# Reordered changes of sub-layer with unread products, half-depth s jobs, pair copies and a shared last norm in a three-part decoder layer

## The chip, the cores and the metric

The kernel runs on one core of one Trainium2 chip. The metric is the time of one execution on the device in microseconds (us). The core has TensorE (PE in the profile, with PEld for the loading of its stationary operand), VectorE (DVE), ScalarE (ACT), GpSimd (POOL) and the queue that issues most transfers (SP). Each engine works through its own instructions in the order written and waits for others at semaphores.

## The reference

One layer with three sub-layers acts on x of 256 tokens by 2048 columns. A conditioning vector c gives a shift, a scale and a gate for each sub-layer through a matrix `w_cond` of 2048 x 18432.

```python
mod = (silu(c) @ w_cond + b_cond).reshape(B, 3, 3, 2048)
u = modulate(x, mod[:, 0, 0], mod[:, 0, 1])            # u = x * (1 + scale) + shift
h = (silu(u @ w1) * (u @ w3)) @ w2                     # FFN1, inner width 5632
x = layer_norm(ALPHA * x + 0.5 * (1 + mod[:, 0, 2]) * h, ln_g[0], ln_b[0])
u = modulate(x, mod[:, 1, 0], mod[:, 1, 1])
q, k, v, s = split(u @ w_in, 4)                        # four times 1024 columns
h = concat([diff_attention(q, k, v, lam), s5_branch(s)]) @ w_out
x = layer_norm(ALPHA * x + (1 + mod[:, 1, 2]) * h, ln_g[1], ln_b[1])
...                                                    # FFN2, like FFN1, with the third rows
```

Everything is float32. The `s5_branch` is a linear recurrence over the tokens in 64 groups with a gated output.

## The kernel before, in words

**Products.** A float32 weight piece of 128 x 1024 (512 KB) is loaded as `raw`, cast by ScalarE to a shorter type as `hi` (L691), and VectorE makes the remainder `lo` = raw - hi. The activations u are kept in the same way as `Uh` and `Ul`, transposed (columns on partitions), in 16 tiles k of 128 columns. A piece is then used in three products per tile: hi with Uh, hi with Ul, lo with Uh. A piece with its products is a job; FFN jobs have 12 products of 512 columns, jobs for s, q and k have 24 of 256 columns. All VectorE and TensorE instructions are recorded through a helper and carry its line, L106 in the profile.

**The order of the work** is written out by the class `Stream`. `run` takes the jobs in order; after each it does what is due (`later(n, f)` puts f behind the n-th job from now) and splits pieces ahead (`split_to`; at most AHEAD = 4 pieces stand in the rings `hi` and `lo`). Jobs marked `hold` split nothing behind them. `pay` issues the low parts that are owed. Between jobs, `drain` puts steps of the conditioning vector (`gv`: a 128 x 1024 product and sum on VectorE) where an account of VectorE's and TensorE's time allows it (LIM, GVM); it rests for the last QUIET jobs of a sub-layer.

**Changes of sub-layer.** The last output block runs its 4 jobs for token half t = 0 first, then for t = 1 in two column halves; `residual` adds gate x product to Y and takes the norm's statistics, `ln_token` ends them (L844), then normalises Y: the first half by ScalarE (L865), the second by VectorE. `turn` transposes pairs of k tiles of Y on TensorE (`ps<-ident,Y`), and `turn_mod` makes `uf` (scale and shift, ScalarE L743), `Uh` and `Ul` of them. Pairs 0 and 1 are turned ahead of the first job of the next sub-layer, the others between the jobs that follow.

**s.** `mk_s(t, hf)` computes 128 columns t of s from half hf of the depth; two t share one PSUM bank. After hf = 1 ScalarE copies the tile out as `sT` (L1147) and issues its transfer to DRAM, `sD`; GpSimd's queue loads it back regrouped as `U` for the recurrence after each fourth t.

**FFN, k-outer.** Part of the w1 and w3 products run pass by pass over the depth and are summed in `kosum`. `up_post` multiplies silu with the up part, and two `turned` steps transpose the result into H.

**Ends.** `z(db)` multiplies Y by the gate and adds ALPHA x (Z_AT gives the jobs). The third sub-layer's norm is two VectorE operations per chunk, then the transfer to the output.

## Time and profile before

| | |
|---|---|
| median of 3 runs | 1914.42 us (1912.57 to 1918.12) |
| profiled execution | 1912.22 us |
| its span | 1910.4 us |
| TensorE busy | 1858.5 us, 97% |
| VectorE busy | 1488.1 us, 78% |
| ScalarE busy | 889.4 us, 47% |
| GpSimd busy | 65.0 us, 3% |
| moved by DMA | 532.36 MB, mean 279 GB/s |

Times in rows count from the start of the span. A row of the timeline has start, duration, engine, line, operation, tiles written and read, shape and number, and in brackets the idle time ahead of it and what ended it. FFN1 runs to about 783 us, the mixer to 1147, FFN2 from there. A product's listed duration overlaps the next one's; the distance of two starts is what a product takes.

### The profile page before, as it was taken

What the parts mean: (1) busy time and instruction counts of PE and PEld (TensorE: products, weight loads), DVE (VectorE), ACT (ScalarE), POOL (GpSimd) and SP (SyncE); (2) the same over time, 40 slices, a digit from 0 to 9 for tenths busy, and PEclk for the clock granted to TensorE, in tenths of its full rate; (3) what the DMA queues carried; (4) which work ended last, traced back from release to release, by engine and by line L of the source; (5) the groups of instructions that cost most, each with busy time, mean ns of one, the idle gap of its engine ahead of it and who ended that gap; (6) DMA issues with size and microseconds to landing.
All of it is one profiled execution on the core that took longest, in us unless ns stands there. A gap on an engine that the chain in (4) does not pass through costs nothing.

```text
span 1910.4 us, 25429 instructions
## 1 busy us (share of the span) xinstructions
PE 1858.5 (97%) x9326; PEld 1567.5 (82%) x9326; DVE 1488.1 (78%) x2255; ACT 889.4 (47%) x1211; POOL 65.0 (3%) x119
## 2 busy tenths in 40 slices
PE   6999999999999999899999998999999999999996
PEld 5888878888888888889999886888888888888885
DVE  6889899978888979888998987887876555445468
ACT  3544444465445433634457635544444444344442
POOL 0000000000000000111210000000000000000000
PEclk9999999999999999999999998999999999999998
DMA  9999878889899888798988885998887555565563
GB/s 375 363 338 315 296 247 292 295 306 309 305 347 326 308 323 312 280 337 294 313 268 311 283 309 202 339 357 275 294 279 249 187 188 191 194 215 187 191 233 110
DMA packets 151935, 532.36 MB, mean 279 GB/s; under 512 B 21841, under 2 KB 23297, under 8 KB 150657
## 3 DMA queue, kind: packets, MB, share of 16 engines
q1 hardware_dynamic: 137234, 495.32, 74.3%
q0 software_dynamic: 6512, 23.89, 3.7%
q10 hardware_dynamic: 8064, 11.54, 1.7%
q8 instruction: 73, 1.20, 0.2%
q14 instruction: 52, 0.43, 0.1%
HBM read 513.34 MB, written 17.33 MB: 278 GB/s over the span
## 4 chain that ended last, share of the span: by engine, by line
PE 87%; DVE 6%; DMA 4%; ACT 2%; issue 1%; POOL 0%; SPq 0%; DVEq 0%; ACTq 0%; POOLq 0%
PE ps L106 87%; DVE lo L106 2%; DVE Y L106 2%; DMA raw<-in_f1w_dram 1%; DVE gv L106 1%; ACT hi L691 1%; DMA early<-in_w_cond_dram 1%; DMA raw<-in_wout_dram 0%; DMA U<-sD 0%; DVE st L106 0%; DVE r L106 0%; DMA sD<-sT 0%; DMA early<-in_wc_dram 0%; ACT Y L865 0%; DVE early L106 0%
## 5 line engine op out<-in xcount | busy, mean ns | idle before, releaser
L106 DVE TENSOR_TENSOR lo<-raw,hi 128x1024 fp32r<-128x1024 f32 x630 | 766.3, 1222 | 342.1 <-ACT hi L691 338.5
L691 ACT CAST hi<-raw 128x1024 fp32r<-128x1024 f32 x630 | 661.4, 1053 | 705.8 <-PE ps L106 461.0
L106 PE MATMUL ps<-hi,Uh 128*128 128x512 f32 x1472 | 583.7, 397 | 16.7 <-ACT Uh L318 9.7
L106 PE MATMUL ps<-hi,Ul 128*128 128x512 f32 x1472 | 577.5, 392 | 0.8 <-DVE Ul L106 0.8
L106 PE MATMUL ps<-lo,Uh 128*128 128x512 f32 x1472 | 457.4, 392 | 1.3 <-DVE lo L106 1.3
L106 PEld LDWEIGHTS ps<-hi,Uh 128*128 128x128 f32 x1472 | 278.7, 189 | 77.8 <-ACT Uh L318 10.4
L106 PEld LDWEIGHTS ps<-lo,Uh 128*128 128x128 f32 x1472 | 278.4, 189 | 60.9 <-DVE lo L106 2.0
L106 PEld LDWEIGHTS ps<-hi,Ul 128*128 128x128 f32 x1472 | 279.0, 190 | 58.1 <-DVE Ul L106 1.9
L106 DVE SCALAR_TENSOR_TENSOR gv<-gv,sc 128x1024 f32<-128x1024 f32 x258 | 314.2, 1219 | 1.4 <-DMA gv<-in_w_cond_dram 1.3
L106 PE MATMUL ps<-hi,Hh 128*128 128x512 f32 (+1 forms) x716 | 274.6, 385 | 0.0
L106 PE MATMUL ps<-hi,Hl 128*128 128x512 f32 (+1 forms) x716 | 273.6, 383 | 0.0
L106 PE MATMUL ps<-lo,Hh 128*128 128x512 f32 (+1 forms) x716 | 216.5, 384 | 1.8 <-DVE lo L106 1.8
L106 PEld LDWEIGHTS ps<-lo,Hh 128*128 128x128 f32 x716 | 133.0, 188 | 29.1 <-DVE lo L106 2.6
L106 PEld LDWEIGHTS ps<-hi,Hh 128*128 128x128 f32 x716 | 134.5, 188 | 26.8 <-issue 0.4
L106 PEld LDWEIGHTS ps<-hi,Hl 128*128 128x128 f32 x716 | 134.6, 188 | 26.0
L106 PE MATMUL ps<-Uh,hi 128*128 128x256 f32 x384 | 97.9, 292 | 2.4 <-ACT sT L1147 1.8
L106 PE MATMUL ps<-Ul,hi 128*128 128x256 f32 x384 | 95.7, 286 | 0.1
L106 PEld LDWEIGHTS ps<-Uh,hi 128*128 128x128 f32 x384 | 74.2, 193 | 6.2 <-ACT sT L1147 2.7
L106 PEld LDWEIGHTS ps<-Ul,hi 128*128 128x128 f32 x384 | 74.2, 193 | 0.8 <-DVE Ul L106 0.7
L1010 ACT CAST Hh<-ps 128x512 fp32r<-128x512 f32 x44 | 25.8, 587 | 78.6 <-PE ps L106 78.6
L106 PE MATMUL ps<-Uh,lo 128*128 128x256 f32 x384 | 53.9, 283 | 0.0
L106 DVE TENSOR_TENSOR Hl<-ps,Hh 128x512 fp32r<-128x512 f32 x44 | 30.3, 688 | 30.0 <-ACT Hh L1010 29.7
(229 smaller groups left out, 1393.4 us busy)
## 6 DMA issues: line engine op xcount, KB each, us to landing
raw<-in_f1w_dram SPq DMA_DIRECT2D x264, 512.0 KB, 6.0
raw<-in_f2w_dram SPq DMA_DIRECT2D x264, 512.0 KB, 4.7
gv<-in_w_cond_dram SPq DMA_DIRECT2D x258, 512.0 KB, 7.1
raw<-in_win_a_dram SPq DMA_DIRECT2D x48, 512.0 KB, 6.0
raw<-in_wout_dram SPq DMA_DIRECT2D x32, 512.0 KB, 5.8
early<-in_w_cond_dram SPq DMA_DIRECT2D x28, 512.0 KB, 7.6
s5m<-scrB POOLq DMA_DIRECT2D x8, 1024.0 KB, 8.4
raw<-in_win_v_dram SPq DMA_DIRECT2D x16, 512.0 KB, 4.8
```

The costliest lines, as they stand in the source:

```text
L106: return f(*a, **k)
L691: S.copy(hi, raw)
L1010: S.copy(hh, p)
```

## The change

It has eight parts.

1. `warm(n)` issues n products of 512 columns whose result nothing reads: 16 in the opening, 11 and 3 behind the transposes of t = 0 and t = 1 at the first change, 12 and 3 at the second.
2. At a change only the first quarter of the second token half is normalised at once; `first_turn` turns two pairs, pays, normalises quarter 1, splits the pieces of the next four jobs and normalises quarters 2 and 3 behind their low parts.
3. The last block splits one piece more, ahead of the first residual; the first piece of a sub-layer gets a slab of its own (`hilo`, listed in `firsts`).
4. The first four s jobs run over k tiles 0 to 3 first, all four of them, and then over 4 to 7; the order of the jobs becomes t 0 to 5 first half, t 0 to 3 second half, t 6 and 7 first half, t 4 to 7 second half. Later pairs are turned one job later.
5. s is copied out for two t at once.
6. In the k-outer passes the second `turned` comes two jobs after the first, not one.
7. Y's gate and ALPHA operations come one and two jobs earlier (Z_AT); QUIET is 6 and 5 for 3; GVM of the mixer 0.68 for 0.65.
8. In the last norm, half of the columns of t = 0 and a quarter of t = 1 are done by ScalarE (one operation) and GpSimd (two); VectorE's last 1024 columns of t = 1 are cut as 512, 256, 256.

Line numbers grow: L106 becomes L110, L691 L705, L743 L757, L865 L887.

TensorE at the first change, in its program around the two turnings (`wr` is the tile that the unread products read; `hilo` the slab of the first piece), before:

```order
2719 L106 MATMUL ps<-lo,Hh 128x256 x2
2720 L106 MATMUL ps<-ident,Y 128x128 x8
2721 L106 MATMUL ps<-Uh,hi 128x256
2722 L106 MATMUL ps<-Ul,hi 128x256
2723 L106 MATMUL ps<-Uh,hi 128x256
```

and after:

```order
2720 L110 MATMUL ps<-lo,Hh 128x256 x2
2721 L110 MATMUL ps<-ident,Y 128x128 x4
2722 L218 MATMUL ps<-wr 128x512 x11
2723 L110 MATMUL ps<-ident,Y 128x128 x4
2724 L218 MATMUL ps<-wr 128x512 x3
2725 L110 MATMUL ps<-Uh,hilo 128x256
```

The unread products stand between the transposes of the two token halves and behind the second.

VectorE at the second change, from the end of the norm's statistics of t = 1, before:

```order
1136 L106 SCALAR_TENSOR_TENSOR rs<-q_10788,rs 128x1
1137 L106 TENSOR_SCALAR Y<-Y,mv,rs 128x512 x4
1138 L106 CAST Uh<-uf 128x256
1139 L106 TENSOR_TENSOR Ul<-uf,Uh 128x256 x2
1140 L106 CAST Uh<-uf 128x256
1141 L106 TENSOR_TENSOR Ul<-uf,Uh 128x256 x2
1142 L106 TENSOR_TENSOR lo<-raw,hi 128x1024
1143 L106 CAST Uh<-uf 128x256
1144 L106 TENSOR_TENSOR Ul<-uf,Uh 128x256 x2
1145 L106 TENSOR_TENSOR lo<-raw,hi 128x1024 x4
```

and after:

```order
1143 L110 TENSOR_SCALAR Y<-Y,mv,rs 128x512
1144 L110 CAST Uh<-uf 128x256
1145 L110 TENSOR_TENSOR Ul<-uf,Uh 128x256 x2
1146 L110 CAST Uh<-uf 128x256
1147 L110 TENSOR_TENSOR Ul<-uf,Uh 128x256 x2
1148 L110 TENSOR_TENSOR lo<-raw,hi 128x1024
1149 L110 TENSOR_SCALAR Y<-Y,mv,rs 128x512
1150 L110 TENSOR_TENSOR lo<-raw,hi 128x1024 x2
1151 L110 TENSOR_SCALAR Y<-Y,mv,rs 128x512 x2
1152 L110 TENSOR_TENSOR lo<-raw,hi 128x1024
1153 L110 SCALAR_TENSOR_TENSOR gv,acc<-gv,sc 128x1024
1154 L110 CAST Uh<-uf 128x256
```

Three of the normalisations have moved behind the first casts and between the low parts, and four low parts now stand ahead of the third pair's cast (row 1154), where one stood.

VectorE at the end of the program, behind the second token half's last `rs`, before:

```order
1452 L106 SCALAR_TENSOR_TENSOR rs<-q_16372,rs 128x1
1453 L106 SCALAR_TENSOR_TENSOR Y<-Y,mv,gb 128x512
1454 L106 SCALAR_TENSOR_TENSOR Y<-Y,rs,bb 128x512
1455 L106 SCALAR_TENSOR_TENSOR Y<-Y,mv,gb 128x512
1456 L106 SCALAR_TENSOR_TENSOR Y<-Y,rs,bb 128x512
1457 L106 SCALAR_TENSOR_TENSOR Y<-Y,mv,gb 128x512
1458 L106 SCALAR_TENSOR_TENSOR Y<-Y,rs,bb 128x512
1459 L106 SCALAR_TENSOR_TENSOR Y<-Y,mv,gb 128x512
1460 L106 SCALAR_TENSOR_TENSOR Y<-Y,rs,bb 128x512
```

and after:

```order
1465 L110 SCALAR_TENSOR_TENSOR nm<-mv,rs 128x1
1466 L110 SCALAR_TENSOR_TENSOR Y<-Y,mv,gb 128x512
1467 L110 SCALAR_TENSOR_TENSOR Y<-Y,rs,bb 128x512
1468 L110 SCALAR_TENSOR_TENSOR Y<-Y,mv,gb 128x512
1469 L110 SCALAR_TENSOR_TENSOR Y<-Y,rs,bb 128x512
1470 L110 SCALAR_TENSOR_TENSOR Y<-Y,mv,gb 128x256
1471 L110 SCALAR_TENSOR_TENSOR Y<-Y,rs,bb 128x256
1472 L110 SCALAR_TENSOR_TENSOR Y<-Y,mv,gb 128x256
1473 L110 SCALAR_TENSOR_TENSOR Y<-Y,rs,bb 128x256
```

One chunk of 512 columns has left VectorE, the last is cut in two, and `nm` (ScalarE's bias) is new.

The diff, cut to its core:

```diff
-GVM = (0.57, 0.65, 0.85, 0.4)
+GVM = (0.57, 0.68, 0.85, 0.4)
...
-Z_AT = (242, 246, 251, 256)
-NOW = (4, 4)
-QUIET = 3
+Z_AT = (242, 246, 250, 254)
+NOW = (4, 1)
+QUIET = (6, 5)
+S_LATER = 2
+WARM = dict(opening=16, mixer=(11, 3), ffn=(12, 3))
 RW = (8, 3, 64)
+LAST = (((1024, 512, True), (1536, 512, True), (0, 1024, False)),
+        ((0, 512, True), (512, 512, False), (1024, 512, False), (1536, 256, False), (1792, 256, False)))
...
+        def warm(n):
+
+            p = psum()
+            for _ in range(n):
+                PE.engine.matmul(p, wr[:, 0:1].to_broadcast([128, 128]), wr.unsqueeze(1).to_broadcast([128, 16, 32]),
+                                 start=True, stop=True)
...
+                warm(WARM["opening"])
...
-                    if len(self.q) - 6 <= self.sp < len(self.q) - 4:
-                        x = pslab("hilo", F32R)
+                    if len(self.q) - 6 <= self.sp < len(self.q) - 4 or self.sp in self.firsts:
+                        x = (slab if self.sp in self.firsts else pslab)("hilo", F32R)
...
+                    stream.split_to(stream.done + 2)
                     residual(0, db, B["pd"][0])
                     ln_token(sub, 0)
...
-                            stream.split_to(stream.done + 2, False)
+                            stream.split_to(stream.done + 3, False)
...
-                w = 512 if t else 1024
-                for c in range(0, D, w):
+                for c, w, pool in LAST[t]:
                     cs = slice(c, c + w)
-                    V.scalar_tensor_tensor(out=Y[:, cs], in0=Y[:, cs], scalar=mv[:, 0:1], in1=gb[:, cs],
-                                           op0=ALU.subtract, op1=ALU.mult)
-                    V.scalar_tensor_tensor(out=Y[:, cs], in0=Y[:, cs], scalar=rs, in1=bb[:, cs],
-                                           op0=ALU.mult, op1=ALU.add)
-                    SP.dma_start(out[t * 128:(t + 1) * 128, cs], Y[:, cs])
+                    E = GP if pool else V
+                    if pool:
+                        S.activation(Y[:, cs], Y[:, cs], AF.Identity, scale=rs, bias=nm)
+                        E.tensor_tensor(Y[:, cs], Y[:, cs], gb[:, cs], op=ALU.mult)
+                        E.tensor_tensor(Y[:, cs], Y[:, cs], bb[:, cs], op=ALU.add)
+                    else:
+                        E.scalar_tensor_tensor(out=Y[:, cs], in0=Y[:, cs], scalar=mv[:, 0:1], in1=gb[:, cs],
+                                               op0=ALU.subtract, op1=ALU.mult)
+                        E.scalar_tensor_tensor(out=Y[:, cs], in0=Y[:, cs], scalar=rs, in1=bb[:, cs],
+                                               op0=ALU.mult, op1=ALU.add)
+                for c, w, pool in sorted(LAST[t], key=lambda x: x[2] and not t):
+                    cs = slice(c, c + w)
+                    (S if pool and t else SP).dma_start(out[t * 128:(t + 1) * 128, cs], Y[:, cs])
...
-        def turn(ks, then):
+        def turn(ks, then, idle=(0, 0)):
...
+                if idle[t]:
+                    warm(idle[t])
+
+        def first_turn(blk, idle):
+
+            turn(range(2), turn_mod(blk), idle)
+            stream.pay()
+            st.pop(("norm", 1, 1))()
+            stream.split_to(stream.done + AHEAD)
+            for q in (2, 3):
+                st.pop(("norm", q, 1))()
...
-                        stream.later(1, lambda: up_post(s, a, 4 * b))
+                        stream.later(1, lambda: up_post(s, a, 4 * b, 2 if b < 3 else 1))
...
-                stream.later(n + 1, lambda: turned(1))
+                stream.later(n + step, lambda: turned(1))
...
+                    def some(p, hi, lo, ks, first):
+                        for k in ks:
+                            w = hi[:, k * 128:(k + 1) * 128]
+                            PE.matmul(p, w, kx(st["U"][0], 8 * hf + k), start=first and k == 0, stop=False,
+                                      skip_group_check=True)
+                            PE.matmul(p, w, kx(st["U"][1], 8 * hf + k), start=False, stop=False, skip_group_check=True)
+                        for k in ks:
+                            PE.matmul(p, lo[:, k * 128:(k + 1) * 128], kx(st["U"][0], 8 * hf + k), start=False,
+                                      stop=hf == 1 and k == 7, skip_group_check=True)
+                    if hf or t >= AHEAD:
+                        some(p, hi, lo, range(8), hf == 0 and t % 2 == 0)
+                        return
+                    some(p, hi, lo, range(4), t % 2 == 0)
+                    M.setdefault("held", []).append((p, hi, lo))
+                    between(t)
+                    if t == AHEAD - 1:
+                        for i, x in enumerate(M.pop("held")):
+                            some(*x, range(4, 8), False)
+                            stream.split_to(stream.done + 2 + i)
 
                 def post():
-                    s = w1([128, 4, 64], "sT")
-                    S.copy(s, M["pt"].rearrange("p (c i) -> p i c", i=4))
-                    if t % 2:
-                        M.pop(("ps", t // 2))
-                    S.dma_start(sD[t * 128:(t + 1) * 128], s)
+                    if t % 2 == 0:
+                        return
+                    p = M.pop(("ps", t // 2))
+                    for i in range(2):
+                        s = w1([128, 4, 64], "sT")
+                        S.copy(s, p[:, i * T:(i + 1) * T].rearrange("p (c i) -> p i c", i=4))
+                        S.dma_start(sD[(t - 1 + i) * 128:(t + i) * 128], s)
...
-                return Job(mm, halves(A["win_a"][t], hf), post if hf else None)
+                return Job(mm, halves(A["win_a"][t], hf), post if hf else None, hold=not hf and t < AHEAD - 1)
...
-            jobs += [mk_s(t, hf) for hf in range(2) for t in range(8)]
+            jobs += [mk_s(t, hf) for ts, hf in (((0, 1, 2, 3, 4, 5), 0), ((0, 1, 2, 3), 1), ((6, 7), 0), ((4, 5, 6, 7), 1))
+                     for t in ts]
...
+        stream.firsts = (len(parts[0]), len(parts[0]) + len(parts[1]))
...
-        turn(range(2), turn_mod(3))
-        mid[2] = lambda: turn((2,), turn_mod(3))
-        mid[4] = lambda: turn((3,), turn_mod(3))
+        first_turn(3, WARM["mixer"])
+        mid[1] = lambda: turn((2,), turn_mod(3))
+        mid[2] = lambda: turn((3,), turn_mod(3))
         for i in range(4):
-            stream.later(1 + i, lambda i=i: turn((4 + i,), turn_mod(3)))
+            stream.later(S_LATER + i, lambda i=i: turn((4 + i,), turn_mod(3)))
...
-        turn(range(2), turn_mod(6))
-        stream.later(0, lambda: turn((2,), turn_mod(6)))
-        stream.later(1, lambda: turn((3,), turn_mod(6)))
+        first_turn(6, WARM["ffn"])
+        stream.later(1, lambda: turn((2,), turn_mod(6)))
+        stream.later(2, lambda: turn((3,), turn_mod(6)))
         for i in range(4):
-            stream.later(2 + i, lambda i=i: turn((4 + i,), kept))
+            stream.later(3 + i, lambda i=i: turn((4 + i,), kept))
```

More of the change, by code (lines that the diff above doesn't have):

```diff
@@ L182, in tile_layer @@
         V.tensor_copy(onesr, ones)
+        wr = sb.tile([128, 32], F32R, tag="wr", name="wr")
+        V.tensor_copy(wr, ident[:, 0:32])
         ch, cl = ([ring.tile([128, CH], F32R, tag=n, name="c" + n, bufs=AHEAD)[0:1, :] for _ in range(2)]
@@ L664, in __init__ @@
                 self.limit = 10 ** 6
-                self.due, self.owed = {}, []
+                self.due, self.owed, self.firsts = {}, [], ()
             def later(self, n, f):
@@ L991, in gated, with up_post, turn_up @@
                 return s
-            def up_post(s, ps, slot):
+            def up_post(s, ps, slot, step=1):
                 for t in range(2):
                     V.tensor_tensor(s[t], s[t], ps[t], op=ALU.mult)
-                turn_up(s, slot)
-            def turn_up(s, slot, n=2):
+                turn_up(s, slot, 2, step)
+            def turn_up(s, slot, n=2, step=1):
                 if slot == 0:
@@ L1133, in mm @@
                         M["ps", t // 2] = psum()
-                    M["pt"] = p = M["ps", t // 2][:, (t % 2) * T:(t % 2 + 1) * T]
-                    for k in range(8):
-                        between(8 * hf + k)
-                        w = hi[:, k * 128:(k + 1) * 128]
-                        PE.matmul(p, w, kx(st["U"][0], 8 * hf + k), start=hf == 0 and k == 0 and t % 2 == 0,
-                                  stop=False, skip_group_check=True)
-                        PE.matmul(p, w, kx(st["U"][1], 8 * hf + k), start=False, stop=False, skip_group_check=True)
@@ L1141, in mm @@
-                    for k in range(8):
-                        PE.matmul(p, lo[:, k * 128:(k + 1) * 128], kx(st["U"][0], 8 * hf + k), start=False,
-                                  stop=hf == 1 and k == 7, skip_group_check=True)
-                def post():
-                    s = w1([128, 4, 64], "sT")
-                    S.copy(s, M["pt"].rearrange("p (c i) -> p i c", i=4))
-                    if t % 2:
-                        M.pop(("ps", t // 2))
-                    S.dma_start(sD[t * 128:(t + 1) * 128], s)
+                    p = M["ps", t // 2][:, (t % 2) * T:(t % 2 + 1) * T]
@@ L1561, in tile_layer @@
         new_stats()
-        stream.run(len(parts[0]) - 4 * NT1 - QUIET)
+        stream.run(len(parts[0]) - 4 * NT1 - QUIET[0])
         drain_s5()
         st["lim"] = None
-        stream.run(QUIET)
+        stream.run(QUIET[0])
         stream.flush()
@@ L1579, in tile_layer @@
         st["lim"], st["gv_max"] = LIM[1], GVM[1]
-        stream.run(len(parts[1]) - QUIET)
+        stream.run(len(parts[1]) - QUIET[1])
         st["lim"] = None
-        stream.run(QUIET)
+        stream.run(QUIET[1])
         stream.flush()
```

6 lines of the change are left out of this document (3 added, 3 removed).

## The prediction, made before the changed kernel was run

> **What bounds the kernel now.** I read the page's busy times and chain first, then what TensorE waited for, then the stretches round its longest waits one by one.
>
> ```profile
> PE 1858.5 (97%) x9326; PEld 1567.5 (82%) x9326; DVE 1488.1 (78%) x2255; ACT 889.4 (47%) x1211; POOL 65.0 (3%) x119
> PE 87%; DVE 6%; DMA 4%; ACT 2%; issue 1%; POOL 0%; SPq 0%; DVEq 0%; ACTq 0%; POOLq 0%
> ...
> PE ps L106 <- ACT Uh L318: 9.7, 2, 7.6
> PE ps L106 <- DVE Y L106: 6.3, 2, 3.2
> ...
> PE ps L106 <- DVE lo L106: 3.6, 4, 1.3
> PE ps L106 <- DVE kosum L106: 3.3, 3, 1.2
> ...
> PE ps L106 <- DMA U<-sD: 2.3, 1, 2.3
> PE ps L106 <- ACT sT L1147: 1.8, 4, 0.5
> ```
>
> TensorE holds 87% of the chain, and the change takes no product away. So what it can win lies in the few places where TensorE waits or runs at half clock, and behind the last product. The waits listed here come to 27.0 us (microseconds; columns: total, times, longest): `ACT Uh` is the opening, `DVE Y` the two changes of sub-layer, `kosum` three stalls in the k-outer passes. The half clock is the second loss; it is seen in the start times of products of one shape:
>
> ```profile
> 1152.88 0.80 PE L106 MATMUL ps<-hi,Uh 128*128 128x512 f32 x1 [0.79 <-DVE Uh L106]
> ...
> 1157.70 0.63 PE L106 MATMUL ps<-hi,Ul 128*128 128x512 f32 x1
> 1158.12 0.63 PE L106 MATMUL ps<-hi,Uh 128*128 128x512 f32 x1
> ...
> 1177.42 0.39 PE L106 MATMUL ps<-hi,Uh 128*128 128x512 f32 x1
> 1177.65 0.39 PE L106 MATMUL ps<-hi,Ul 128*128 128x512 f32 x1
> ```
>
> Two starts lie 0.42 us apart at 1158 and 0.23 at 1177: a product of 512 columns costs 0.19 more when cold, one of 256 columns about half of that.
>
> **Second change (mixer to FFN2): the largest term.** Before, only the first job's piece was split when the work began. The stretch reads:
>
> ```profile
> 1147.47 0.60 PE L106 MATMUL ps<-ident,Y 128*128 128x128 f32 x4
> ...
> 1156.25 1.22 PE L106 MATMUL ps<-lo,Uh 128*128 128x512 f32 x2 [1.27 <-DVE lo L106]
> ...
> 1163.38 0.79 PE L106 MATMUL ps<-hi,Uh 128*128 128x512 f32 x1 [2.49 <-ACT hi L691]
> ...
> 1175.14 0.60 PE L106 MATMUL ps<-ident,Y 128*128 128x128 f32 x4
> 1175.49 0.48 PE L106 MATMUL ps<-hi,Uh 128*128 128x512 f32 x1
> ```
>
> Jobs 0 to 3 (twelve products each) and their turnings run from 1152.88 to 1175.49, 22.6 us. Warm and unhindered they are 48 products at 0.23 and four turnings at 0.35 (1175.14 to 1175.49), 12.4: at most 10.2 can be won. The change attacks all three parts: the unread products fill the 3.23 (12 x 0.23 = 2.8 if they stay warm), the pieces of jobs 0 to 3 are split before these start (the 2.49 and 1.27 go), and three of the four normalisations of the second token half move behind low parts. VectorE's new queue is then the limit, and its prices are
>
> ```profile
> 786.11 2.04 DVE L106 TENSOR_SCALAR Y<-Y,mv,rs 128x512 f32<-128x512 f32 x4
> 788.07 0.28 DVE L106 CAST Uh<-uf 128x256 fp32r<-128x256 f32 x1
> 788.38 0.96 DVE L106 TENSOR_TENSOR Ul<-uf,Uh 128x256 fp32r<-128x256 f32 x2
> ...
> 795.01 4.64 DVE L106 TENSOR_TENSOR lo<-raw,hi 128x1024 fp32r<-128x1024 f32 x4 [0.52 <-ACT hi L691]
> ```
>
> Counted: four quarters 2.04, two pairs at 1.24, four low parts 4.64, in all 9.2 us from about 1150.2. The fourth low part is ready at some 1159.5, before job 3 needs it (1152.9 + 3 x 2.8 = 1161.2); the normalised quarters of pairs 2 and 3 come between, so their turnings may sit a little late. I take -9.8. If the clock is not kept, 48 products at 0.42 replace the 0.23 for about 5 us (12 of them, +2.3), and if the low parts are late by the two waits seen here (1.27 + 2.49, of which I keep two thirds) another 2.5: bounds -5 and -10.2.
>
> **First change (FFN1 to mixer).**
>
> ```profile
> 786.71 1.11 PE L106 MATMUL ps<-ident,Y 128*128 128x128 f32 x4 [3.06 <-DVE Y L106]
> 788.40 0.58 PE L106 MATMUL ps<-Uh,hi 128*128 128x256 f32 x1 [0.58 <-DVE Uh L106]
> ...
> L1147 ACT COPY sT<-ps x8: 372/372/373, 820.7 to 843.7; 128x256 f32<-128x256 f32 x8
> ...
> 1146.75 0.28 PE L106 MATMUL ps<-hi,Ah 128*128 128x256 f32 x1
> ...
> 1147.23 0.40 PE L106 MATMUL ps<-lo,Ah 128*128 128x256 f32 x2
> ...
> 799.24 1.02 ACT L743 ACTIVATE uf<-ps,bt,gs 128x256 f32<-128x256 f32 x2 [1.32 <-PE ps L106]
> ```
>
> The columns of the copy's row are min, median and max in ns, then the first and last start. Products of 256 columns start 0.12 us apart: six lie between 1146.75 and the 1147.47 quoted above. The s phase, 16 jobs of 24, is 46.1 us of products and six turnings of 0.35; it lasted from 788.40 to 843.7, 55.3 us. Some 7.1 are lost. Of these the wait for the copy sT is 1.8 in the row above; counted as the copy's whole 0.37 and as much again until products run, it is 4 x 0.73 = 2.9. Copies in pairs, each after both halves of a bank are complete, take it away. The rest, about 4.2, is the clock and the wait for pairs 2 and 3. The half-depth order (four jobs over pairs 0 and 1 first) fills these waits with 48 products at 0.12 = 5.8 us, but the deep turnings then come one job later each, and turning 7 stands directly ahead of the first job that reads it: its chain is 1.02 (two uf on ScalarE) + 0.28 + 0.96 = 2.3, and nothing covers it. Of the 4.2 I count 2.6 as won. So -2.9 - 2.6 + 2.3 = -3.2; bounds -6 (the new stall is covered) and +1 (it is doubled by VectorE's queue and nothing is won of the clock). VectorE is full there, so a bound near the bad end is real:
>
> ```profile
> 797.00:820.00 23.00, 23.00 (x195) 23.00 (x194) 22.55 (x40) 13.58 (x20) 0.00 (x0) 1.00 0.92 331
> 820.00:850.00 30.00, 25.86 (x208) 24.87 (x207) 25.89 (x30) 12.44 (x17) 2.59 (x4) 1.00 0.99 344
> ```
>
> (columns: stretch, its length, busy time and count of PE, PEld, DVE, ACT, POOL, granted clock, DMA share, GB/s.) Whether the idle before turning 7 also costs the clock is open: behind the wait of 3.06 it did (four transposes 1.11, against 0.60 at 1175.14). I take the wait alone, since it is shorter; else it is some 2.5 more, inside the bounds.
>
> **The wait for U, 2.3 us,** goes: its data are the s values of tiles 0 to 3, whose last halves now run two jobs (2 x 2.9) earlier. -2.3; 0 if the DMA engines, 0.99 busy in that stretch, land it late all the same.
>
> **The opening.** Sixteen unread products stand behind the first shift product, in the 7.6 us that TensorE waits for `Uh`.
>
> ```profile
> 22.75 0.79 PE L106 MATMUL ps<-hi,Uh 128*128 128x512 f32 x1 [7.59 <-ACT Uh L318]
> ...
> 28.59 0.46 PE L106 MATMUL ps<-hi,Ul 128*128 128x512 f32 x1
> ...
> 38.86 0.74 PE L106 MATMUL ps<-hi,Uh 128*128 128x512 f32 x1 [2.09 <-ACT Uh L318]
> ...
> 28.60:38.90 10.30, 8.21 (x37) 6.47 (x35) 9.74 (x17) 3.63 (x6) 0.00 (x0) 1.00 1.03 408
> ```
>
> From 22.75 to 28.59 TensorE runs cold, 2.7 us lost. But at 38.86 it waits for data again, with the DMA engines full (1.03) and VectorE busy 9.74 of 10.3. What is won before that wall is waited for at it. I take 0; bounds -2.7 and +0.5.
>
> **Three smaller ones.** *k-outer:* the second product of each new group waited for `kosum` of the group just ended, 1.1 us three times (the row above); with the second turning one job later this wait comes a job later.
>
> ```profile
> 249.00:281.00 32.00, 28.67 (x133) 22.75 (x133) 28.12 (x40) 16.08 (x22) 0.00 (x0) 1.00 0.67 234
> ```
>
> VectorE is busy 28.12 of 32.00 there, so its work would fit without the stalls, but with no slack for a bad order. By setting the jobs out by hand I find 0.65 of each 1.1 left, at both turnings: 3 x 0.45 saved, -1.4 (0 to -3.3). *Y before low parts:* two of the four waits on `lo` (3.6 together) stand behind Y operations which now run one and two jobs earlier, ahead of the end of either FFN; they are half of the row, -1.8 (0 to -1.8).
>
> **Last norm.** Behind the last product VectorE alone holds the chain:
>
> ```profile
> 1891.10 1.28 DVE L106 SCALAR_TENSOR_TENSOR Y<-Y,mv,gb 128x1024 f32<-128x1024 f32 x1
> ...
> 1896.13 0.42 DVE L106 TENSOR_TENSOR r<-ps,G 128x256 f32<-128x256 f32 x1
> ...
> 1905.23 0.75 DVE L106 SCALAR_TENSOR_TENSOR Y<-Y,rs,bb 128x512 f32<-128x512 f32 x1
> ...
> L592 POOL TENSOR_TENSOR ks<-ks,s5f 128x32 f32<-128x32 f32 x8 | 3.2, 397 | 231.3 <-ACT ks L591 231.3
> ...
> L1192 POOL MEMSET s5e<- 128x512 f32 x2 | 1.1, 536 | 81.2 <-PE ps L106 81.2
> ```
>
> Four operations of 1024 ran from 1891.10 to 1896.13; two of them leave VectorE ahead of the second half's residual, but TensorE's last product lets that start only some 1.6 us earlier; two of eight 512-operations leave it too, 1.1 net (the last 1024 columns are cut finer). -2.7, if ScalarE and GpSimd hurt nobody. A GpSimd operation on 512 columns with two inputs has no row: at least 0.54 (a memset of that size), at most 16 x 0.4 = 6.4 by the small one. I take 1.2 (0.4 and twice the memset's slope), nearer to the row of its own size; six of them then end well before VectorE. Against VectorE's operations they may collide, so I take -1.5, nearer to -2.7 than to the loss of rival 2 below, +3.6, since VectorE's queue has its own waits in which GpSimd fits.
>
> **Sum:** -9.8 - 3.2 - 2.3 + 0 - 1.4 - 1.8 - 1.5 = -20.0 us. The profiled execution took 1912.22 (span 1910.4 and 1.8 round it), 2.2 below the median of 1914.42; the sum laid on the median gives 1894.4.
>
> **Rivals.** (1) *VectorE is the wall at both changes.* For: 22.55 of 23.00 in the row above, and its work is not less. Against: at the second change its counted 9.2 us stand against 12.4 of products. Then the first change gives 0 and the second 5, with the rest as above: -12.0, 1902.4. (2) *The last norm costs.* If GpSimd and VectorE exclude each other there, VectorE's operations (14.9 us from 1891.10 to the end of the row at 1905.23, less 2.5 and 1.1) and six GpSimd operations of 1.2 stand in a row: 18.5 for 14.9, +3.6 where I have -1.5: 1899.5. Against: no row of before has them side by side, so it is open. The Trainium skill ("SBUF — State Buffer", "SBUF: two separate sides") says that a VectorE operation with two SBUF inputs and a GpSimd operation that reads SBUF take one lock, and the second waits for the whole of the first; by that rule this rival is the case and the sum is -14.9, without it -21.2. No run so far shows which. (3) *The gain at the first change is paid back to the transfers:* the DMA engines are 0.92 to 0.99 busy until 850, U and the pieces land no earlier, -14.5, 1899.9. (4) *Slower: an unread product is dear.* It reads a 32-column tile repeated by a zero step, which no row of before shows. 29 of them stand on the path at the two changes, over the 6.3 us of waits on Y, and 16 in the opening over the 7.6 on `Uh`. At p us each they add 45p - 13.9. To be 5.7 slower in all they must eat 25.7: from p = 0.88, twice the cold 0.42, this decides. At p = 1.2 they add 40, 1934. Against: the type and size are those of their neighbours. (5) *The change does not do what it says:* the clock falls in spite of the unread products, since they end before the real ones start; each change loses the 2.7 that the opening lost, -14.6, 1899.8.
>
> **How the numbers follow.** The forecast, 1894.4, has 0.55; rival (1) 0.17, (2) 0.10, (3) 0.06, (5) 0.08, (4) 0.04. The forecast's own range, with its terms partly at either end, is 1888 to 1899. All good ends together give about 1884, all bad ones some 1912. I state 1887 to 1904, which takes rivals (1), (2), (3) and (5) in. A measurement of this kernel tells about 0.3% from none, 5.7 us: faster means under 1908.7. Of the forecast and rivals without (4), some 0.07 falls short of that: faster 0.88, same 0.08, slower 0.04.
>
> **What would show it.** In the changed profile: no wait of PE on Y over 1 us at either change, and products of 512 columns 0.23 apart from the first job of FFN2; the fourth job's end there some 12 to 13 us after the first one's start. The wait on sT and on U gone from TensorE's list, a new one on Uh or Ul of about 2 us just ahead of the second half-depth jobs. The wait at 38.86 still at its place and longer. GpSimd's operations near 1.2 us, VectorE's of 512 still 0.75 beside them. The forecast falls if the second change wins less than 6 us, or if the last output lands over 14 us after the last product.

## The result, and the profile after

| | median | range | runs |
|---|---|---|---|
| before | 1916.27 us | 1912.57 to 1920.72 | 4 |
| changed | 1900.28 us | 1898.42 to 1903.10 | 4 |

The ratio is 0.992, with a 95% interval of 0.9897 to 0.9943: 10.9 to 19.7 us faster, 15.3 by the ratio. The forecast was 20.0 faster, 1894.4, with a range from 1887 to 1904. The two profiled executions lie nearer together, 1912.22 and 1900.65 (spans 1910.4 and 1898.9), because that of before was among its fastest; the terms below are measured between these two.

The page of the changed kernel (busy times, chain) and what its TensorE waited for:

```profile
PE 1866.8 (98%) x9371; PEld 1574.0 (83%) x9371; DVE 1488.4 (78%) x2256; ACT 891.3 (47%) x1214; POOL 74.8 (4%) x125
PE 87%; DVE 7%; DMA 4%; ACT 1%; issue 1%; ACTq 0%; SPq 0%; POOL 0%; DVEq 0%
...
PE ps L110 <- ACT Uh L332: 4.3, 2, 2.6
PE ps L110 <- ACT chi L193: 3.6, 1, 3.6
PE ps L110 <- DVE Uh L110: 2.2, 1, 2.2
PE ps L110 <- DMA s5e<-scrA: 1.7, 1, 1.7
PE ps L110 <- DVE kosum L110: 1.6, 6, 0.3
PE ps L110 <- DVE Y L110: 1.1, 2, 0.7
...
PE ps L110 <- DVE lo L110: 0.4, 1, 0.4
```

The waits on Y (6.3 to 1.1), sT, U, hi and lo have gone or shrunk. Two are new at their place: on `DVE Uh`, 2.2, and on the transfer `s5e`, 1.7, which no part of the prediction names.

To see where the time went I matched the 9326 products that both kernels have, by their rank in the program, and took the difference of their start times.

| place | predicted | measured, profile against profile |
|---|---|---|
| opening | 0 | +0.8 |
| k-outer turning | -1.4 | -1.35 |
| 290 to 770, nothing changed there | | +0.65 |
| Y ahead of low parts, both ends of an FFN | -1.8 | -2.2 |
| first change and s phase | -3.2 | -1.9 |
| wait for U | -2.3 | -2.5 |
| wait for s5e and the clock behind it, 925 to 938 | none | +5.0 |
| second change, to the 49th product of FFN2 | -9.8 | -10.1 |
| the rest of the mixer and of FFN2 | | +0.6 |
| last product to the end of the span | -1.5 | -0.6 |
| all | -20.0 | -11.6 |

The second change, in the timeline of the changed kernel:

```profile
1146.45 0.60 PE L110 MATMUL ps<-ident,Y 128*128 128x128 f32 x4
1146.81 3.07 PE L218 MATMUL ps<-wr 128*128 128x512 f32 x12
1150.28 0.66 PE L110 MATMUL ps<-ident,Y 128*128 128x128 f32 x4 [0.40 <-DVE Y L110]
1150.70 0.95 PE L218 MATMUL ps<-wr 128*128 128x512 f32 x3
...
1164.04 0.60 PE L110 MATMUL ps<-ident,Y 128*128 128x128 f32 x4
```

From the first transposes to the product behind the fourth job it takes 17.9 us, where it took 28.0 (1147.47 to 1175.49). The unread products take 0.23 each (12 by 1150) and no wait over 0.4 is left. Of the 10.1 us, 0.35 is a turning that now comes behind that product instead of ahead of it, so 9.7 are won. Before, the two waits behind the first job took 3.8 (1.27 and 2.49), and the clock was at half for almost the whole stretch (0.51, third from the end of this row of the kernel before):

```profile
1152.00:1169.00 17.00, 12.45 (x32) 8.84 (x32) 9.72 (x16) 7.75 (x13) 0.00 (x0) 0.51 0.27 85
```

In the changed kernel it is 1.00 there. What the waits and the turning leave of the 10.1, some 6, goes for the most part with this half clock: the 24 products of 512 columns in that row start 0.43 apart and not 0.23, which makes 4.8.

What was lost again stands at 927. TensorE's row there in the changed kernel (the bracket is the idle time ahead and its releaser):

```profile
927.25 3.23 PE L110 MATMUL ps<-U,s5e 128*128 128x64 f32 x16 [1.70 <-DMA s5e<-scrA]
```

GpSimd's queue ahead of it:

```profile
919.87 0.54 POOL L315 DMA_DIRECT2D growD<-grow  x1 [14.79 <-DVE grow L110]
920.39 0.57 POOL L1240 DMA_DIRECT2D s5e<-scrA  x1
```

The chain of waits that ended last in that stretch (start, duration, what):

```profile
919.39 0.20 DVE grow L110
919.59 0.28 issue
919.87 0.46 POOL growD L315
920.32 0.07 issue
920.39 6.81 DMA s5e<-scrA
927.20 0.04 issue
927.25 7.82 PE ps L110 x38
```

The ten us behind it (columns as in the prediction's windows, the clock third from the end):

```profile
928.00:938.00 10.00, 10.00 (x60) 9.23 (x60) 5.99 (x13) 1.97 (x5) 0.00 (x0) 0.67 0.95 337
```

And the kernel before: GpSimd's queue, and TensorE's first product with that load:

```profile
919.13 0.54 POOL L301 DMA_DIRECT2D growD<-grow  x1 [8.24 <-DVE grow L106]
919.66 0.57 POOL L1194 DMA_DIRECT2D s5e<-scrA  x1
931.21 1.90 PE L106 MATMUL ps<-U,s5e 128*128 128x64 f32 x16
```

GpSimd's queue loads the next matrices of the recurrence (`s5e`). In the same queue, ahead of that load, stands the store of the mixer's gate row (`growD`), which waits for VectorE's conditioning stream. That stream ends where it ended before, 919.9 against 919.1, while TensorE arrives 5.8 us earlier than it did. The load takes 6.8 us; before, TensorE came for it 11.5 us after its issue (931.21), now it waits 1.7, and behind the wait the clock is 0.67 in the ten us from 928. The transfer itself has a share: before, the same load took 4.8 us, and with that it would have landed at 925.2, just ahead of TensorE at 925.55.

### The profile page after: what moved, and what is told of

It reads as the page before. It is cut to its first block, busy times and chain, and to the rows that moved or that the text cites. A ratio compares the mean times of both kernels' runs of the same rounds, so it can differ in the third digit from the quotient of the medians.

```text
span 1898.9 us, 25539 instructions
## 1 busy us (share of the span) xinstructions
PE 1866.8 (98%) x9371; PEld 1574.0 (83%) x9371; DVE 1488.4 (78%) x2256; ACT 891.3 (47%) x1214; POOL 74.8 (4%) x125
## 4 chain that ended last, share of the span: by engine, by line
PE 87%; DVE 7%; DMA 4%; ACT 1%; issue 1%; ACTq 0%; SPq 0%; POOL 0%; DVEq 0%
PE ps L110 87%; DVE lo L110 2%; DVE gv L110 2%; DVE Y L110 1%; DMA raw<-in_f1w_dram 1%; DMA early<-in_w_cond_dram 1%; DVE kosum L110 1%; DMA gv<-in_w_cond_dram 1%; DMA scrB<-tabr 1%; ACT hi L705 0%; DMA raw<-in_wout_dram 0%; DMA s5e<-scrA 0%; DMA early<-in_wc_dram 0%; ACT Y L887 0%; DVE st L110 0%
## 5 line engine op out<-in xcount | busy, mean ns | idle before, releaser
L110 DVE TENSOR_TENSOR lo<-raw,hi 128x1024 fp32r<-128x1024 f32 x628 | 763.8, 1222 | 334.3 <-ACT hi L705 332.4
L705 ACT CAST hi<-raw 128x1024 fp32r<-128x1024 f32 x628 | 659.1, 1053 | 703.6 <-PE ps L110 481.9
L110 PE MATMUL ps<-hi,Uh 128*128 128x512 f32 x1468 | 580.1, 395 | 4.4 <-ACT Uh L332 4.3
L110 PE MATMUL ps<-hi,Ul 128*128 128x512 f32 x1468 | 574.7, 391 | 1.1 <-DVE Ul L110 1.1
L110 PE MATMUL ps<-lo,Uh 128*128 128x512 f32 x1468 | 454.0, 391 | 0.0
L110 PEld LDWEIGHTS ps<-hi,Uh 128*128 128x128 f32 x1468 | 277.1, 189 | 63.9 <-ACT Uh L332 5.3
L110 PEld LDWEIGHTS ps<-lo,Uh 128*128 128x128 f32 x1468 | 276.7, 188 | 58.8
L110 PEld LDWEIGHTS ps<-hi,Ul 128*128 128x128 f32 x1468 | 277.2, 189 | 57.6 <-DVE Ul L110 1.7
L110 DVE SCALAR_TENSOR_TENSOR gv<-gv,sc 128x1024 f32<-128x1024 f32 x258 | 314.5, 1220 | 1.9 <-DMA gv<-in_w_cond_dram 1.4
L110 PE MATMUL ps<-hi,Hh 128*128 128x512 f32 (+1 forms) x716 | 274.6, 385 | 0.0
L110 PE MATMUL ps<-hi,Hl 128*128 128x512 f32 (+1 forms) x716 | 273.7, 383 | 0.0
L110 PE MATMUL ps<-lo,Hh 128*128 128x512 f32 (+1 forms) x716 | 216.3, 383 | 0.0
L110 PEld LDWEIGHTS ps<-hi,Hh 128*128 128x128 f32 x716 | 134.5, 188 | 26.6 <-issue 0.4
L110 PEld LDWEIGHTS ps<-hi,Hl 128*128 128x128 f32 x716 | 134.6, 188 | 26.2
L110 PEld LDWEIGHTS ps<-lo,Hh 128*128 128x128 f32 x716 | 133.1, 188 | 26.6
L110 PE MATMUL ps<-Uh,hi 128*128 128x256 f32 x376 | 95.3, 290 | 2.2 <-DVE Uh L110 2.2
L110 PE MATMUL ps<-Ul,hi 128*128 128x256 f32 x376 | 93.3, 285 | 0.1
L110 PEld LDWEIGHTS ps<-Uh,hi 128*128 128x128 f32 x376 | 72.7, 193 | 5.1 <-issue 2.6
L110 PEld LDWEIGHTS ps<-Ul,hi 128*128 128x128 f32 x376 | 72.8, 194 | 0.3 <-DVE Ul L110 0.3
L110 DVE TENSOR_TENSOR Hl<-ps,Hh 128x512 fp32r<-128x512 f32 x44 | 30.3, 689 | 32.0 <-ACT Hh L1043 32.0
L110 PE MATMUL ps<-Uh,lo 128*128 128x256 f32 x376 | 53.2, 283 | 0.0
```

What stands on the lines that cost most here:

```text
L110: return f(*a, **k)
L705: S.copy(hi, raw)
```

## The experiments

Each but the last two was run once with a profile; a time is given beside the changed kernel's 1898.9 of span, and places are compared within the profiles, since the spans of single executions differ by some 2 us for reasons outside the edit (the first `Uh` alone came between 21.9 and 24.2 us in the fourteen profiles).

**The gate row's store moved to SP.**

```diff
-                GP.dma_start(growD[sub:sub + 1, i * 1024:(i + 1) * 1024]...
+                SP.dma_start(growD[sub:sub + 1, i * 1024:(i + 1) * 1024]...
```

> The gate row's store (growD) is issued by SP instead of GpSimd; nothing else is changed. Theory Q (GpSimd's queue): in the changed kernel TensorE waited 1.7 us at 927 for s5e, whose load stood in GpSimd's queue behind the gate row's store until 919.87, and then ran cold to 937, 5.0 us in all. Without the store in that queue the load goes out some 14 us earlier, at 905: no wait on s5e, the profiled span falls by about 5 us, to 1894. Theory D (the transfers themselves are late, since the DMA engines are full there): the wait stays, within 1 us of 1.7, span 1898 to 1900. A load of raw behind the store on SP could wait for VectorE: less than 1 us, as four pieces are loaded ahead.

GpSimd's queue in this run, and the window behind:

```profile
905.19 2.22 POOL L1243 DMA_DIRECT2D s5e<-KD  x4
907.40 0.56 POOL L1240 DMA_DIRECT2D s5e<-scrA  x1
```

```profile
928.00:938.00 10.00, 10.00 (x88) 9.60 (x87) 9.95 (x19) 3.73 (x8) 0.00 (x0) 1.00 0.91 320
```

The load goes out at 907.40 instead of 920.39, the wait on s5e is gone and the clock stays at 1.00: between the products on either side of 925 to 940 the run gains 5.1 us. Theory Q holds: the load itself took 9.8 us here, longer than in the changed kernel, and no wait came of it, since it was issued in time. The span, 1896.7, fell by only 2.2, because 1.5 were lost behind the wait on Uh at 812 (below), 0.9 ahead of the first change and 0.4 at the end of the program. In the nine other runs below that have this wait, it was 0.2 to 2.8 us; it cost 0.5 to 2.2 where the clock stayed, and 5.4 to 6.0 where the clock fell (5.0 in the changed kernel): it is a race of two streams that a small shift decides.

**No unread products at the changes.**

```diff
-WARM = dict(opening=16, mixer=(11, 3), ffn=(12, 3))
+WARM = dict(opening=16, mixer=(0, 0), ffn=(0, 0))
```

> The unread products are left out at both changes of sub-layer, the 16 in the opening stay. Theory C (they keep the clock): the first products of either sub-layer start 0.42 us (512 columns) and 0.21 (256) apart for some 5 us; FFN2 begins with products 2.5 us later by its fourth job, the mixer 1 to 2.5, though part is caught up by VectorE's queue there. Span +3 to +5. Theory S (the earlier split does the work, the unread products nothing): span within 1 us of the changed kernel's 1898.9.

```profile
1144.43 1.12 PE L110 MATMUL ps<-ident,Y 128*128 128x128 f32 x4 [3.23 <-DVE Y L110]
1146.10 0.80 PE L110 MATMUL ps<-hilo,Uh 128*128 128x512 f32 x1 [0.56 <-DVE Uh L110]
```

The transposes are cold again (1.12 for four, against 0.66). The second change takes 20.1 us instead of 17.9, the first loses 1.2 by its 49th product. So theory C, at its lower end: the unread products are worth 3.4 us in all, not the larger part. The span, 1895.2, is lower than the changed kernel's for other reasons: this execution had an opening 1.9 us earlier and a wait on s5e of 0.6.

**No unread products in the opening.**

```diff
-                warm(WARM["opening"])
```

> The 16 unread products of the opening are left out. Theory N (they end 2.6 us before Uh comes, and the clock is lost again): products from 23 us on start 0.42 apart in both, span within 1 us; TensorE's wait on Uh is 7.6 as before the change. Theory L (they delay Uh, which came 1.0 later in the changed kernel): first product at 22.75, span 1.0 lower. If they had kept the clock: span up to 2.7 higher.

The first product came at 22.87, TensorE waited 7.75 for it, and its clock was low till 29, as in the kernel before. What decides is another number. From the first product to the 49th, at which the next `Uh` is waited for, it takes 15.85 us here; in the twelve other profiles with the change 15.84 to 15.86, and 16.11 in the kernel before, whether the clock was low at first (13.8 us to the start of the 48th product in the changed kernel) or not (11.5 in the run without unread products at the changes, where `Uh` came as the unread products of the opening ended). Theory N, and with it the wall that the prediction put there: the 16 products bring nothing, even when they keep the clock. Theory L falls, though the first product did come early here: in all fourteen profiles the first product starts 4.34 or 4.35 us behind the start of VectorE's third operation on `early`, which waits for a transfer, and no work of TensorE stands in between.

**The last norm by VectorE alone, and GpSimd in t = 0 alone.** The first edit takes ScalarE and GpSimd out of both token halves, the second out of t = 1.

```diff
-LAST = (((1024, 512, True), (1536, 512, True), (0, 1024, False)),
-        ((0, 512, True), (512, 512, False), ...
+LAST = (((0, 1024, False), (1024, 1024, False)),
+        ((0, 512, False), (512, 512, False), ...
```

> The last norm is done by VectorE alone again, the output of the second half in the changed kernel's pieces. The changed kernel's end took 14.07 us from the start of the last product to the end of the span, before it 14.69. Theory P (VectorE and GpSimd lock each other out): VectorE's operations of 512 columns are 0.75 again, of 1024 1.28, of 256 with two SBUF inputs 0.43, instead of 1.75, 2.20 and 1.06; the end then takes 14.0 to 14.7, so that ScalarE and GpSimd have brought less than 1 us. Theory F (no lock, only slow GpSimd): VectorE's operations keep their lengthened durations without GpSimd, and the end takes over 15.5.

```diff
-        ((0, 512, True), (512, 512, False), (1024, 512, False), ...
+        ((0, 512, False), (512, 512, False), (1024, 512, False), ...
```

> Of the last norm ScalarE and GpSimd keep only their half of t = 0; t = 1 is VectorE's alone. By the lock, VectorE's operations of 512 columns behind the last rs take 0.75 again, not 1.75 and 1.63: from that rs to VectorE's last operation 6.4 us instead of 6.9 (8 operations by 0.72 or 0.50 each for the halves, two more than now), so the end from the last product takes 13.4 to 13.8 against 14.07. Without a lock there it would be 14.8, as the two operations come on top.

The changed kernel's VectorE, then its GpSimd:

```profile
1881.66 2.20 DVE L110 SCALAR_TENSOR_TENSOR Y<-Y,rs,bb 128x1024 f32<-128x1024 f32 x1
1883.78 0.41 DVE L110 TENSOR_TENSOR r<-ps,G 128x256 f32<-128x256 f32 x1
1884.22 1.06 DVE L110 TENSOR_TENSOR Y<-r,Y 128x256 f32<-128x256 f32 x1
...
1890.19 1.75 DVE L110 SCALAR_TENSOR_TENSOR Y<-Y,mv,gb 128x512 f32<-128x512 f32 x1
1891.98 1.63 DVE L110 SCALAR_TENSOR_TENSOR Y<-Y,rs,bb 128x512 f32<-128x512 f32 x1
```

```profile
1881.36 1.41 POOL L872 TENSOR_TENSOR Y<-Y,gb 128x512 f32<-128x512 f32 x1 [193.62 <-ACT Y L871]
1882.85 2.16 POOL L873 TENSOR_TENSOR Y<-Y,bb 128x512 f32<-128x512 f32 x1
```

And VectorE in the first of the two runs, without GpSimd beside it:

```profile
1882.90 1.28 DVE L110 SCALAR_TENSOR_TENSOR Y<-Y,rs,bb 128x1024 f32<-128x1024 f32 x1
...
1884.56 0.42 DVE L110 TENSOR_TENSOR Y<-r,Y 128x256 f32<-128x256 f32 x1
...
1889.72 0.75 DVE L110 SCALAR_TENSOR_TENSOR Y<-Y,mv,gb 128x512 f32<-128x512 f32 x1
```

The same operations take 1.28, 0.42 and 0.75 alone, and 2.20, 1.06 and 1.75 beside GpSimd, each longer by 0.15 to 0.2 less than what was left of the GpSimd operation beside it (0.92 of 1.11, 0.64 of 0.79, 1.00 of 1.20). The one that reads PSUM and a single SBUF tile, `r<-ps,G`, takes 0.41 in both. GpSimd's operations stretch too, 2.16 for 1.41. That is theory P, and the rule that the prediction cited from the Trainium skill ("SBUF — State Buffer", "SBUF: two separate sides"): the traces agree, also in that one SBUF input doesn't lock. From the last product to the end it takes 14.95 us with VectorE alone, 14.07 as changed (13.75 to 14.46 in the ten profiles with that end) and 13.29 with GpSimd in t = 0 alone (13.68 in the version with three edits below). These totals hold the last output transfer and the end of the program, which vary; both runs missed their expected ends by 0.1 to 0.25 (14.95 for at most 14.7, 13.29 for at least 13.4). VectorE's part is steadier. From the start of the last product to the end of VectorE's last operation it is 11.00 us with VectorE alone, 10.63 or 10.64 in the ten profiles as changed, 10.20 or 10.21 with GpSimd in t = 0 alone, and 10.23 in the kernel before. So sharing t = 0 pays 0.8 there and sharing t = 1 costs 0.4, since VectorE has no idle time in t = 1 in which GpSimd's operations could fit.

**Turnings 4 to 7 one job earlier.**

```diff
-S_LATER = 2
+S_LATER = 1
```

> The turnings of pairs 4 to 7 come one job earlier than in the changed kernel (as far behind the jobs as before the change). Theory T (turning 7 stands bare ahead of the first job that reads it): the wait of 2.2 us on Uh at 812 in the changed kernel goes, and with it the half clock that followed it in three of five profiles; span -2 to -4 against the changed kernel's 1898.9. Theory V (VectorE is the wall from 797 to 820): a wait of about 2 us on lo, Ul or Uh appears elsewhere before 830, span within 1 us.

VectorE of the changed kernel ahead of `Uh` at 812, and the TensorE row that waited for it:

```profile
808.60 1.22 DVE L110 TENSOR_TENSOR Y<-Y,gb 128x1024 f32<-128x1024 f32 x1
809.74 1.22 DVE L110 TENSOR_TENSOR lo<-raw,hi 128x1024 fp32r<-128x1024 f32 x1
810.87 1.22 DVE L110 SCALAR_TENSOR_TENSOR gv<-gv,sc 128x1024 f32<-128x1024 f32 x1
...
812.02 0.29 DVE L110 CAST Uh<-uf 128x256 fp32r<-128x256 f32 x1
```

```profile
812.36 0.38 PE L110 MATMUL ps<-Uh,hi 128*128 128x256 f32 x1 [2.22 <-DVE Uh L110]
```

The window behind it in the changed kernel, and the same in the run with the store on SP:

```profile
813.00:818.00 5.00, 5.00 (x42) 4.96 (x43) 5.00 (x7) 1.42 (x2) 0.00 (x0) 1.00 0.94 303
```

```profile
813.00:818.00 5.00, 4.73 (x24) 4.49 (x25) 4.97 (x8) 1.05 (x1) 0.00 (x0) 0.66 0.90 268
```

`Uh` of turning 7 stands behind Y's scaling, a low part and a conditioning step on VectorE. With the earlier turning the wait on it is gone, but 1.37 us on Y appear at 796 and the 49th product comes 2.0 later than as changed. The s phase's 384 products, from the first transposes of the change, take 57.3 us; as changed they take 58.6, or 60.0 where the clock fell behind the wait (60.5 before). So the edit is worth 1.3 to 2.7: theory T, with half of its gain lost to VectorE, as theory V has it. The span, 1893.6, is 5.3 lower, mostly because this run has no wait on s5e: its gate row is stored 2.0 us before the last product of the recurrence's batch (917.72 against 919.70), where it came 1.1 behind it.

The 2.2 us cost the clock in six of the eleven profiles that have them (0.66 in the row above), 1.5 us, and not in the others (1.00). The Trainium skill ("TensorE: Matmul & The Clock Gate", Part 1, "What's actually happening") describes a free-running window of about 3.4 us, and a low clock after an idle one: that a wait of one length has both outcomes agrees with a free-running window, but neither an idle time of 2.2 us nor the 1.7 at 927 fills such a window, and both were followed by the low clock.

**s copied out one tile at a time.**

```diff
-                    if t % 2 == 0:
-                        return
-                    p = M.pop(("ps", t // 2))
-                    for i in range(2):
+                    p, i = M["ps", t // 2], t % 2
...
```

> s is copied out tile by tile again; the order of the s jobs and all else is the changed kernel's. Theory B (a copy of one half of a bank holds up the products into the other): four waits on sT of about 0.5 come back and the s phase is 2.9 us longer; span +2.9 less what is caught up later. Theory O (the new order of the jobs removed them): no wait on sT, span within 1 us.

Four waits on sT of 0.5, 1.8 in all, are back as in the row quoted of before, and the phase takes 62.7 us against 60.0 of the runs whose clock fell in the same place: 2.7. Theory B.

**Late split, one piece split, and all quarters at once, at the second change.** The first leaves out the `split_to` ahead of job 0 for jobs 2 and 3 (its expectation counts job 1 in, whose piece the last block still splits), the second that for job 1 too; the third normalises t = 1 whole at both changes.

```diff
             st.pop(("norm", 1, 1))()
-            stream.split_to(stream.done + AHEAD)
+            if blk == 3:
+                stream.split_to(stream.done + AHEAD)
```

> At the second change the pieces of jobs 1 to 3 aren't split ahead of job 0; the unread products, the late normalisations and the first change stay. Theory A (the early split is the larger part of the 9.8 us won there): the wait on ScalarE's hi comes back behind job 0 (2.5 us before) and the clock is lost with it, span +4 to +7. Theory C (the kept clock is the larger part): a wait of under 1.5 us with the clock at 1.00, span +1 to +2.

```diff
-                            stream.split_to(stream.done + 3, False)
+                            stream.split_to(stream.done + (2 if sub == 1 else 3), False)
...
```

> At the second change only the piece of job 0 is split ahead, as in the kernel before; the run that split two pieces lost under 1 us, so the question is the second piece. Unread products and late normalisations stay. Theory A (job 1's early split is needed): TensorE waits behind job 0 for ScalarE's hi, about 2 us, since the cast then starts with job 0's end or later, and FFN2's fourth job ends 2 to 5 us later than in the changed kernel. Theory C (the kept clock and the late normalisations carry the 9.8 us): under 1 us.

```diff
-NOW = (4, 1)
+NOW = (4, 4)
...
```

> All four quarters of t = 1 are normalised at once at both changes, ahead of the first casts, as in the kernel before; nothing is normalised late. Theory Y (the late quarters let the casts of pairs 0 and 1 start earlier): three more quarters of 0.5 stand ahead of the transposes, so TensorE's wait on Y grows by 1.2 to 1.6 us at each change; the span by 1.5 to 3, less where VectorE is the wall behind it (first change). Rival: VectorE has the same work in all, so the wait on Y grows but the later jobs catch up, span within 1 us.

Measured from the first transposes to the 49th product of FFN2: 17.9 as changed, 17.9 without the split of jobs 2 and 3, 18.7 with job 0's piece alone, 18.5 with all quarters at once (theory Y, at half its price: the wait on Y grew by 0.5, not 1.2 to 1.6, and at the first change nothing was lost by the 49th product). Theory A falls in both runs; in the first, though, ScalarE's order is the changed kernel's, cast by cast, and only two low parts of VectorE change places with two quarters, so it tests no later cast. The second moves one cast. The reason stands in ScalarE's queue. First the kernel before, then the run with one piece split:

```profile
1153.15 1.02 ACT L743 ACTIVATE uf<-ps,bt,gs 128x256 f32<-128x256 f32 x2
1154.20 0.41 ACT L745 CAST Uh<-uf 128x256 fp32r<-128x256 f32 x1
1160.92 1.02 ACT L743 ACTIVATE uf<-ps,bt,gs 128x256 f32<-128x256 f32 x2 [6.32 <-PE ps L106]
1161.97 0.40 ACT L745 CAST Uh<-uf 128x256 fp32r<-128x256 f32 x1
1162.29 3.88 ACT L691 CAST hi<-raw 128x1024 fp32r<-128x1024 f32 x4
```

```profile
1150.33 0.41 ACT L759 CAST Uh<-uf 128x256 fp32r<-128x256 f32 x1
1150.64 3.90 ACT L705 CAST hi<-raw 128x1024 fp32r<-128x1024 f32 x4
1156.36 1.02 ACT L757 ACTIVATE uf<-ps,bt,gs 128x256 f32<-128x256 f32 x2 [1.82 <-PE ps L110]
```

Before, pair 2 was turned behind job 0, ahead of the split behind that job; its `uf` waited 6.32 us for TensorE's transposes, and four casts stood behind it. Now the turning comes a job later, and the casts go at once even where nothing is split early. By the order of the program either edit gets the casts past the waiting `uf`. That the later turning alone carries the larger part is read from these rows and not shown: a run with the early split and the old turning wasn't made.

**Three edits together.** The store on SP, turnings one job earlier and the last norm's t = 1 on VectorE alone, each as above; beside it the changed kernel unaltered, five rounds on the same chip.

> Three edits on the changed kernel together: the gate row's store issued by SP, turnings 4 to 7 one job earlier, the last norm's t = 1 by VectorE alone. By the single runs: 0.4 to 5 for the s5e wait (it differed from run to run), 2.2 to 3.5 for the bare turning with its clock, 0.8 for the end: -3.5 to -8 against the changed kernel of the same call, some 1894 where that one has 1900. If they overlap (earlier turnings already avoid the s5e wait): -3 to -4.

> The changed kernel unaltered, beside the version with three edits: 1898 to 1903, ratio to the kernel before 0.990 to 0.994. In its profile the wait on s5e is between 0 and 2 us, as in the other runs that left that part alone.

| | median | range | ratio to before |
|---|---|---|---|
| before | 1916.33 | 1909.69 to 1918.96 | |
| changed | 1900.05 | 1895.75 to 1906.49 | 0.9921 (0.9902 to 0.9939) |
| three edits | 1894.82 | 1893.54 to 1896.77 | 0.9894 (0.9877 to 0.9911) |

The three edits bring another 5.2 us by the medians, as expected; the intervals overlap, and one run of the changed kernel lies among those of the edited one. It is the fastest version here by its median, but the one run with the earlier turnings alone, 1895.35, lies in its range, so what each edit adds isn't shown. Its runs spread less (3.2 us for 10.7). The race for s5e is out of it, but that this is the reason isn't shown: the kernel before, without a wait there in its profile, spreads by 9.3. The unaltered kernel's wait on s5e was 2.75, not the 0 to 2 expected.

## Why the prediction was right, and where its steps were not

The time lies inside the range and the largest term was right in size; the sum was 4 to 5 us too good by the medians, and 8.4 between the two profiles from which the terms are measured. The prediction's ends for all good and all bad terms, 1884 and 1912, come out of its own bounds as 1885.4 and 1914.5; nothing hangs on that. Five steps were measured close to what was written: k-outer (-1.35 for -1.4), Y ahead of the low parts (-2.2 for -1.8, beyond its bound of -1.8, since the two waits were worth more than half of the row), the wait for U (-2.5 for -2.3), the copies in pairs (2.7 for 2.9) and the bare turning 7 (2.2 for 2.3). Of the other signs written down, the waits on Y (0.72 and 0.40), the 0.23 between products and the end of FFN2's fourth job (12.7 us behind the first one's start) came too.

*The wall of the opening* was right and is shown: 15.85 us from the first `Uh` to the second, whatever the clock. The +0.8 comes from the first `Uh`, which hangs on a transfer. The sign that the wait at 38.86 would grow didn't come (1.66 for 2.09): the unread products ended too early to keep the clock. Where it was kept, the wait was 3.95 to 3.97.

*The step that failed* is the sum: it adds up the terms as if what is won at the first change and at U stayed won, and has no term for a load that this makes late. I priced each wait at its place and followed none of them downstream. The page's first fence showed no wait on s5e, so it did not occur to me that 11.5 us lay between a load's issue and its use only because TensorE was late. The added pace met a load whose issue hangs on VectorE's stream, through GpSimd's queue; it gave back 5.0 us in this profile. Rival (3) had the gain of the first change paid back, but to full DMA engines; the run with the store on SP shows that the queue decides: with the engines 0.91 busy (0.95 in the changed kernel) the wait went. The slower transfer, 6.8 us for 4.8, is what is left of rival (3).

*First change:* -1.9 for -3.2. The copies and the new wait were as counted, so it is the rest of the sum that was too large: of the 4.2 us of clock and waits I had 2.6 as won, and 1.3 were. In runs where the clock falls behind turning 7 hardly anything is left of the term (60.0 against 60.5), which was the 2.5 that I left within the bounds; it is 1.5.

*Second change:* the size was right (-10.1 for -9.8, or -9.7 with the turning counted in both), and so was where the time lay, 3.8 in the two waits and most of the rest in the clock; what takes it away was not. I gave the early split the two waits and the unread products the clock. By the runs that leave one part out, the unread products carry 2.2, the split of job 1's piece 0.8, the late quarters 0.6. Without the unread products the clock was at half for 6.8 us, in the kernel before for 17.1: so they aren't what ended most of it. The rest, some 6, I put down to the order in ScalarE's queue, which I hadn't read: the row of the wait names `hi`, and `hi` itself waited behind a `uf` that waited for TensorE. No run takes this order back alone, so it stays argued.

*Last norm:* -0.6 for -1.5, and that it lies between the two bounds is luck. VectorE, to which the term gave 2.7 less or 3.6 more, ends its last operation 0.4 later behind the last product than before (10.63 for 10.23). The -0.6 comes behind it, in the last transfer, which is half as large now, and in the end of the program; there the ten profiles with this end differ by 0.7 among themselves. GpSimd's operation took 1.4 where 1.2 was taken, and VectorE's of 512 columns beside it up to 1.75, where the sign written down was 0.75. Rival (2), the lock, is the mechanism, but not at its price: the operations collide only where both engines are busy. The sign by which the forecast falls, an output over 14 us behind the last product, is met by the end of the span (14.07), but not by the landing of the last transfer (12.6). *Rival (4)*, a dear unread product, is excluded: 0.23 warm. *Rival (1)* and *(5)* didn't come; the clock held at both changes.

## What to carry to other kernels

When an edit lets the bounding engine run ahead, look past its own place: list the loads that are issued by in-order queues, and for each the time between its issue and its use; a load with little slack, queued behind something that doesn't move with the edit, is where the gain goes. A wait on an engine's output isn't explained by that engine's duration: look at what stood ahead in its queue. And an operation moved to an idle engine must be priced beside its neighbours: here the operations of two engines lengthened each other, and the part on the critical stretch cost more than it gave.

## What the runs showed of the hardware that I had not expected

A wait of TensorE of 2.2 us was followed by half the clock for 3.4 us in six of eleven profiles and by the full clock in five, at the same place of nearly the same program. At 927 a wait of 1.7 us was followed by half the clock in the changed kernel, and one of 1.9 in the run without the split of jobs 2 and 3 was not. Waits of 3.1 to 3.3 us were, at both changes of the kernel before and of the run without unread products. In the clock that the fourteen traces record, every stretch at half speed that begins and ends between 20 us and the last product lasted 3.41, 6.83 or 17.07 us: one, two or five times 3.41. VectorE's operation with one PSUM and one SBUF input ran at its usual 0.41 us beside GpSimd, while those with two SBUF inputs of the same size took 1.06 instead of 0.42.
